# Modulation products on TensorE in pairs of tiles, in the state space stage of a two-layer trunk

## The chip, the cores and the metric

The kernel runs on one core of one Trainium2 chip. The metric is the device time of one execution in microseconds, of which the median over several runs is compared. Engines are called as the profile calls them: PE is TensorE's matmuls and PEld its weight loads, DVE is VectorE, ACT is ScalarE, POOL is GpSimd, and SP is SyncE, whose queue issues most of the DMAs.

## What is computed

Two layers over 256 latent tokens of width 1024, with 256 context tokens that layer 0 reads. All of it is in float32. Layer 0 mixes tokens with a bidirectional state space scan (Mamba-2), layer 1 with a convolution module; each is followed by a gated feed-forward part. Ahead of every part the tokens are normalised and modulated by vectors that come from a condition `c`:

```
def ada_params(sc, w, b):          # sc = silu(c)
    mod = sc @ w + b               # (1, 1024) @ (1024, 6144)
    return [t[:, None, :] for t in jnp.split(mod, 6, axis=-1)]

for i in range(DEPTH):
    sh1, s1, g1, sh2, s2, g2 = ada_params(sc_lat, ada_w[i], ada_b[i])
    xn_lat = modulate(rmsnorm(h_lat, norm_mix_g[i]), sh1, s1)   # h * (1 + scale) + shift
    y_lat = ssd_mixer(...) if i == 0 else conformer_conv_module(...)
    h_lat = h_lat + g1 * y_lat
    h_lat = h_lat + g2 * swiglu(modulate(rmsnorm(h_lat, norm_ffn_g[i]), sh2, s2), ffn_w_in[i], ffn_w_out[i])
```

In the state space mixer `h @ w_in` gives a gate z, the inputs x, B and C of the scan, and its steps dt. x, B and C pass a short convolution and SiLU; then eight groups of four heads each are scanned, and the result goes through the gate, a norm and `w_out`.

The six vectors of a layer have 1024 values each; one vector is the product of silu(c) with a 1024x1024 block of `ada_w`.

## The kernel before, in words

Every large matmul is done in three passes over operands split into a high and a low part (`mm3`, L281 to L283). A weight tile of 128x1024 (or 128x768) comes through `weights` (L266): SP's queue loads it into a raw buffer `wraw`, ACT casts it to the high part `wh` (L273), DVE subtracts to get the low part `wl` (L274), and PE multiplies both. The raw buffers are a ring of four (`wr`, WR = 4), the pairs `wh` and `wl` a ring of four as well. A raw buffer of a weight tile is free when the subtraction is done.

The kernel is a sequence of stages: the modulation of the first norm and the first projections (`ssd_in`, to about 56 us), the state space stage (`ssd`, to about 285 us), the projection through `w_out`, the feed-forward part, the convolution module, and the second feed-forward part.

In the state space stage the eight groups are worked off with one group's projection ahead of the scan of the group before. A group's projection is four weight tiles of `w_xb`; every second group also takes four tiles of `w_z`, every fourth four tiles of `w_c`. A `w_xb` tile feeds 18 matmuls of 128x512, a `w_z` or `w_c` tile 12. The scan of a group loads 1.5 MB of decays (`emat`, L873) and 0.5 MB more (`eo`, L878), works on them on ACT and DVE, and uses products on halves of PE's columns (L951, L959).

The vectors that are needed after this stage are computed inside it, as background work. `self.bg` holds three of them (the mixer's gate, and shift and scale of the feed-forward part; `vector` with `on_pe`). Each call of `weights` adds `self.rate` to a credit, and whenever the credit reaches one, `background` takes one step of the list. A step of `vector` loads one tile of 128x1024 of `ada_w` into a buffer of the same ring `wr` (L344), and multiplies it as it is, in float32, by silu(c) (`ada_mm`, L330): four matmuls, each with 32 columns of stationary values and 256 columns of the tile, at four places beside each other in PE's columns (`tile_position=(0, 32 * j)`). They add up in a bank `pa` over the eight tiles of a vector; then ACT copies the bank out (L316), PE transposes it and DVE adds the bias (L324). The trace has two records for each of these float32 matmuls. A raw buffer of a modulation tile is free when its four matmuls are done. With 0.6 for the rate, the 24 tiles of the three vectors are spread over 40 weight tiles.

In stage 1 the function `quarter` uses the same `ada_mm` (tiles named `araw`) on loads that hold two values of k, with 128 columns for each matmul. Its products for k and k + 1 stand behind each other.

No order is written out by hand for this stage: a scheduler places the instructions of each engine by priority and readiness, with the loads of `ada_w` and of weights raised by 100 (`high_priority(AHEAD)`).

Of the kernel before, what the change touches and what calls it, by code (L numbers as in the profile page):

```python
# [8 lines left out]
F32 = mybir.dt.float32  # L9
# [7 lines left out]
P = 128  # L17
D = 1024
KD = D // P
# [203 lines left out]
class Trunk:  # L223
# [101 lines left out]
                                    in1=bias.rearrange("p (j q) -> p j q", j=4), op=ALU.add)  # L325
        return col

    def ada_mm(self, pa, k, rhs, n):
        for j in range(4):
            self.nc.tensor.matmul(out=pa[32 * j:32 * j + 32, 0:n], lhsT=self.sc[:, k, :], rhs=rhs(j),  # L330
                                  start=k == 0, stop=k == KD - 1, tile_position=(0, 32 * j))

    def vector(self, l, i, on_pe):


        nc, t = self.nc, self.t
        c = PC_AB + l * 48 + i * KD
        bias = self.pc[:, c:c + KD]
        if on_pe:
            pa = self.pa.tile([P, 512], F32, name="pa")  # L340
            for k in range(KD):
                raw = self.wr.tile([P, 1024], F32, name="wraw")
                with self.tc.high_priority(AHEAD):
                    nc.sync.dma_start(out=raw, in_=t["ada_w"][l, k * P:(k + 1) * P, i * D:(i + 1) * D])  # L344
                self.ada_mm(pa, k, lambda j: raw[:, j * 256:j * 256 + 256], 256)
                if k < KD - 1:
                    yield
            col = self.ada_columns(pa, 256, 1, bias)
        else:
            if self.srow is None:  # L350
                self.silu_row()
            col = self.sb.tile([P, KD, 1], F32, name="ada_col", bufs=12)
            for k in range(KD):
                raw = self.ar.tile([P, 1024], F32, name="araw")
                with self.tc.high_priority(AHEAD):
                    nc.sync.dma_start(out=raw, in_=t["ada_wt"][l * 6 + i - 5, k])
                self.flight.append((raw, col, k, (l, i, bias) if k == KD - 1 else None))

                if len(self.flight) >= AR:
                    self.land()  # L360
                yield
            return
        self.done(l, i, col)
        yield
# [456 lines left out]
    def ssd(self, es, xh, xl):  # L821
        nc, t, tc = self.nc, self.t, self.tc
        pd, pa0 = self.ssd_in(xh, xl)
        self.bg = [self.vector(0, i, True) for i in range(2, 5)]
        self.rate = 0.6
        sp_ = es.enter_context(tc.tile_pool(name="ssd", bufs=1))
        sqacc = sp_.tile([P, 2, L], F32, name="sqacc")
        nc.gpsimd.memset(sqacc, 0.0)
# [406 lines left out]
```

## Time and profile before

| what | value |
|---|---|
| median of 3 runs | 884.21 us (881.93 to 885.55) |
| the profiled execution: its own time | 882.65 us |
| its span, first to last instruction | 880.8 us |
| mean granted clock of PE | 0.991 |
| bytes moved | 194.59 MB, 221 GB/s |
| tiles of `ada_w` that come through the ring | 24, 512 KB each, median 4.1 us from issue to landing |

A row of a group of instructions names line, engine, operation and what it writes and reads (out<-in by the program's names, the moving operand first), then how many, and in ns the duration of one. A row of the order of time has start and duration in us and a count of records that were merged. A row of waits says who waited for whom, how long in total, how often, and the longest. SPq is SP's queue of DMA issues. Ends of matmuls are modelled in the trace, so a later start behind a record says more than its end.

### The profile page before, as it was taken

The page shows a single profiled execution, that of the slowest core. Times are in us where ns is not written, and L with a number is a line of the kernel's source. Part 1 is how long each engine was busy: PE and PEld are TensorE (multiplying, and loading weights), DVE is VectorE, ACT ScalarE, POOL GpSimd, SP SyncE. Part 2 cuts the span into 40 slices and gives each one's busy share as a digit, 9 for nine tenths or more (in the row PEclk, how much of TensorE's full clock was granted, in tenths as well). Part 3 has the DMA queues.
Part 4 walks back from the last instruction along what each step waited for, and adds up shares of the span by engine and source line. Part 5 has one row for each costly group of instructions (what it writes and reads, how often), then busy time and mean ns, then how long its engine had stood idle before and what let it go on. Part 6 is the DMA issues. An engine that isn't in the chain of part 4 may idle for free.

```text
span 880.8 us, 12563 instructions
## 1 busy us (share of the span) xinstructions
PE 845.3 (96%) x4555; PEld 645.0 (73%) x4555; DVE 663.6 (75%) x1093; ACT 506.8 (58%) x852; POOL 49.9 (6%) x78
## 2 busy tenths in 40 slices
PE   6999999999999999989999999999989999999996
PEld 3676766767677777767888877877767788888885
DVE  2469588896878989889889888668987896555434
ACT  3376887796767978467244444566354645444421
POOL 1001001101010010120000000010000000000000
PEclk8999999999999999999999999999999999999998
DMA  9747856657563454468899889836655697555521
GB/s 346 312 144 245 288 167 216 239 159 246 157 203 127 161 191 146 160 215 275 288 395 382 333 292 346 286 108 227 169 167 169 220 329 264 182 177 190 191 72 48
DMA packets 55873, 194.59 MB, mean 221 GB/s; under 512 B 6666, under 2 KB 9170, under 8 KB 54787
## 3 DMA queue, kind: packets, MB, share of 16 engines
q1 hardware_dynamic: 54338, 190.00, 62.9%
q0 software_dynamic: 896, 2.28, 0.7%
q10 hardware_dynamic: 576, 1.51, 0.5%
q8 instruction: 36, 0.59, 0.3%
q14 instruction: 27, 0.21, 0.1%
HBM read 191.94 MB, written 1.82 MB: 220 GB/s over the span
## 4 chain that ended last, share of the span: by engine, by line
PE 46%; DVE 4%; DMA 3%; ACT 3%; issue 1%; POOL 0%; SPq 0%; POOLq 0%; ACTq 0%; DVEq 0%
PE acc L283 14%; PE acc L282 14%; PE acc L281 14%; DVE wl L274 2%; PE ps L250 2%; DMA wraw<-in_ffn_out_dram 2%; DMA wraw<-in_w_pw_dram 1%; ACT wh L273 1%; PE ps L1094 1%; ACT modv L147 1%; DMA wraw<-in_ffn_in_dram 1%; ACT nrm L94 0%; DVE araw L370 0%; DVE xml L287 0%; DVE nrm L107 0%
## 5 line engine op out<-in xcount | busy, mean ns | idle before, releaser
L274 DVE TENSOR_TENSOR wl<-wraw,wh 128x1024 fp32r<-128x1024 f32 (+2 forms) x230 | 270.3, 1181 | 99.7 <-ACT wh L273 98.7
L273 ACT CAST wh<-wraw 128x1024 fp32r<-128x1024 f32 (+2 forms) x230 | 232.0, 1017 | 167.5 <-PE acc L283 63.0
L281 PE MATMUL acc<-wh,xmh 128*128 128x512 f32 x544 | 219.2, 403 | 2.4 <-ACT bx L704 1.7
L283 PE MATMUL acc<-wh,xml 128*128 128x512 f32 x544 | 214.9, 395 | 0.4 <-DVE xml L287 0.4
L282 PE MATMUL acc<-wl,xmh 128*128 128x512 f32 x544 | 214.9, 395 | 0.4 <-DVE wl L274 0.4
L281 PEld LDWEIGHTS acc<-wh,xmh 128*128 128x128 f32 x544 | 102.5, 188 | 30.8 <-issue 5.2
L283 PEld LDWEIGHTS acc<-wh,xml 128*128 128x128 f32 x544 | 102.4, 188 | 24.7 <-DVE xml L287 2.0
L282 PEld LDWEIGHTS acc<-wl,xmh 128*128 128x128 f32 x544 | 102.6, 189 | 21.8 <-DVE wl L274 1.0
L281 PE MATMUL acc<-xmh,wh 128*128 128x512 f32 (+1 forms) x200 | 80.7, 403 | 0.0
L282 PE MATMUL acc<-xml,wh 128*128 128x512 f32 (+1 forms) x200 | 79.2, 396 | 0.0
L283 PE MATMUL acc<-xmh,wl 128*128 128x512 f32 (+1 forms) x200 | 78.8, 395 | 0.3 <-DVE wl L274 0.3
L711 DVE SCALAR_TENSOR_TENSOR bx<-bxraw,pc,bx 128x508 f32<-128x508 f32 (+1 forms) x96 | 67.7, 742 | 5.9 <-ACT bx L704 5.7
L282 PE MATMUL acc<-wl,midh 128*128 128x512 f32 x176 | 69.5, 395 | 0.4 <-DVE wl L274 0.3
L283 PE MATMUL acc<-wh,midl 128*128 128x512 f32 x176 | 69.1, 393 | 0.0
L370 DVE SCALAR_TENSOR_TENSOR araw<-araw,srow 128x1024 f32<-128x1024 f32 x56 | 68.1, 1218 | 1.0 <-DMA araw<-in_ada_wt_dram 0.9
L281 PE MATMUL acc<-wh,midh 128*128 128x512 f32 x176 | 66.1, 395 | 0.4 <-ACT wh L273 0.4
L281 PEld LDWEIGHTS acc<-xmh,wh 128*128 128x128 f32 (+1 forms) x200 | 37.2, 186 | 13.6 <-issue 5.1
L283 PEld LDWEIGHTS acc<-xmh,wl 128*128 128x128 f32 (+1 forms) x200 | 37.1, 186 | 9.7 <-issue 1.2
L282 PEld LDWEIGHTS acc<-xml,wh 128*128 128x128 f32 (+1 forms) x200 | 37.2, 186 | 8.7 <-issue 1.9
L282 PEld LDWEIGHTS acc<-wl,midh 128*128 128x128 f32 x176 | 33.0, 188 | 9.5 <-DVE wl L274 2.1
L281 PEld LDWEIGHTS acc<-wh,midh 128*128 128x128 f32 x176 | 32.9, 188 | 8.2 <-ACT wh L273 1.0
L283 PEld LDWEIGHTS acc<-wh,midl 128*128 128x128 f32 x176 | 33.0, 188 | 7.3
(203 smaller groups left out, 1063.0 us busy)
## 6 DMA issues: line engine op xcount, KB each, us to landing
wraw<-in_ffn_in_dram SPq DMA_DIRECT2D x88, 512.0 KB, 5.0
araw<-in_ada_wt_dram SPq DMA_DIRECT2D x56, 512.0 KB, 5.0
wraw<-in_ffn_out_dram SPq DMA_DIRECT2D x44, 512.0 KB, 3.8
wraw<-in_w_xb_dram SPq DMA_DIRECT2D x32, 384.0 KB, 3.9
wraw<-in_ada_w_dram SPq DMA_DIRECT2D x24, 512.0 KB, 4.1
emat<-edram SPq DMA_DIRECT2D x8, 1536.0 KB, 7.8
wraw<-in_w_pw_dram SPq DMA_DIRECT2D x24, 512.0 KB, 4.5
araw<-in_ada_dram SPq DMA_DIRECT2D x16, 512.0 KB, 7.8
```

Of the source, the lines that this page charges most:

```text
L147: j = self.nc.scalar.activation(out=v[:, i], in_=y, func=AF.Identity, scale=g, bias=b)
L250: self.nc.tensor.transpose(out, in_, self.ident[0:n, 0:n])
L273: nc.scalar.copy(out=wh[:r, :n], in_=raw[:r, :n])
L274: nc.vector.tensor_tensor(out=wl[:r, :n], in0=raw[:r, :n], in1=wh[:r, :n].bitcast(F32), op=ALU.subtract)
L281: mm(out=out, lhsT=ah, rhs=bh, start=first, stop=False)
L282: mm(out=out, lhsT=ah, rhs=bl, start=False, stop=False)
L283: mm(out=out, lhsT=al, rhs=bh, start=False, stop=last)
L370: self.nc.vector.scalar_tensor_tensor(out=raw, in0=raw, scalar=1.0, in1=self.srow, op0=ALU.mult, op1=ALU.mult, accum_out=col[:, k])
L711: nc.vector.scalar_tensor_tensor(out=o[:, :, a:b], in0=r[:, :, a + d:b + d], scalar=w(k), in1=o[:, :, a:b], op0=ALU.mult, op1=ALU.add)
L1094: nc.tensor.matmul(out=x[32 * g:32 * g + 32], lhsT=dk[:, blk - 1, g * 8 + i], rhs=rows(u4[:, g])[:, r0:r0 + nr, 4 * i:4 * i + 64], start=i ...
```

## The change

A step of the background work in the state space stage now takes two tiles. Both loads are issued behind each other, and the products of both stand behind each other, those of the later tile first. The first and last product of a sum in PSUM are marked accordingly: tile 1 opens the sum and tile 6 closes it. A vector takes four steps instead of eight, and the rate is 0.3 instead of 0.6, so that the 12 steps are spread over the same 40 weight tiles. The ring keeps its four buffers. Lines behind the change are four higher than before.

```
-    def ada_mm(self, pa, k, rhs, n):
+    def ada_mm(self, pa, k, rhs, n, ends=(0, KD - 1)):
         for j in range(4):
             self.nc.tensor.matmul(out=pa[32 * j:32 * j + 32, 0:n], lhsT=self.sc[:, k, :], rhs=rhs(j),
-                                  start=k == 0, stop=k == KD - 1, tile_position=(0, 32 * j))
+                                  start=k == ends[0], stop=k == ends[1], tile_position=(0, 32 * j))
...
             pa = self.pa.tile([P, 512], F32, name="pa")
-            for k in range(KD):
-                raw = self.wr.tile([P, 1024], F32, name="wraw")
+            for kp in range(KD // 2):
+                raw = [self.wr.tile([P, 1024], F32, name="wraw") for _ in range(2)]
                 with self.tc.high_priority(AHEAD):
-                    nc.sync.dma_start(out=raw, in_=t["ada_w"][l, k * P:(k + 1) * P, i * D:(i + 1) * D])
-                self.ada_mm(pa, k, lambda j: raw[:, j * 256:j * 256 + 256], 256)
-                if k < KD - 1:
+                    for a in range(2):
+                        k = 2 * kp + a
+                        nc.sync.dma_start(out=raw[a], in_=t["ada_w"][l, k * P:(k + 1) * P, i * D:(i + 1) * D])
+
+                for a in (1, 0):
+                    self.ada_mm(pa, 2 * kp + a, lambda j: raw[a][:, j * 256:j * 256 + 256], 256, (1, KD - 2))
+                if kp < KD // 2 - 1:
                     yield
...
         self.bg = [self.vector(0, i, True) for i in range(2, 5)]
-        self.rate = 0.6
+        self.rate = 0.3
```

## The prediction

> **What bounds the kernel now.** I read the busy times of the page first, then the window of the stage that the change touches, then the order of time inside it, and last who waits there.
>
> ```profile
> PE 845.3 (96%) x4555; PEld 645.0 (73%) x4555; DVE 663.6 (75%) x1093; ACT 506.8 (58%) x852; POOL 49.9 (6%) x78
> core 0: us, PE busy (x) PEld busy (x) DVE busy (x) ACT busy (x) POOL busy (x), PEclk, DMA share, GB/s
> 56.00:285.00 229.00, 224.38 (x1266) 161.59 (x1265) 185.94 (x329) 173.92 (x322) 18.09 (x16) 1.00 0.63 204
> ```
>
> TensorE is busy for 96% of the span. From 56 to 285 us, the stretch of the state space stage that holds the products of the change, it is busy 224.38 of 229 us at full clock (PEclk 1.00), so only 4.62 us are idle. VectorE is busy 81% of it, ScalarE 76%, the DMA engines 63%. TensorE is the bound, and what shortens its queue shortens the stage as long as the others keep up. A busy TensorE need not be at its peak, so the next view is its order of time around one run of modulation products; the columns are start, duration, instruction and count.
>
> ```profile
> 59.12 0.39 PE L282 MATMUL acc<-wl,xmh 128*128 128x512 f32 x1
> 59.35 0.40 PE L283 MATMUL acc<-wh,xml 128*128 128x512 f32 x1
> 59.68 0.64 PE L330 MATMUL pa<-wraw,sc 128*32 128x256 f32 x8
> 60.24 0.50 PE L281 MATMUL acc<-wh,xmh 128*128 128x512 f32 x1
> 60.58 0.39 PE L282 MATMUL acc<-wl,xmh 128*128 128x512 f32 x1
> ```
>
> The matmuls of a projection start 0.23 us apart (59.12 to 59.35). One modulation tile, four products in the code and eight records in the trace, each on a quarter of the array's columns, stands between 59.35 and 60.58, which is 1.23 us. Two ordinary steps would be 0.46 us. A run therefore costs 1.23 - 0.46 = 0.77 us.
>
> How much of that is the products themselves?
>
> ```profile
> L330 PE MATMUL pa<-wraw,sc x192: 379/391/403, 59.7 to 257.0; 128*32 128x256 f32 x192
> ```
>
> The first numbers are the shortest, median and longest in ns. Eight records of 0.39 us fit into 0.64 us, so they run side by side; the last starts 0.64 - 0.39 = 0.25 us after the first. They come as two packs of four, one pack each 0.25 us. Two packs are 0.50 us, and 0.77 - 0.50 = 0.27 us is the price of going from the whole array to quarters and back, paid once for each run, whatever its length.
>
> Stage 1 has longer runs, which tell whether the packs keep their pace.
>
> ```profile
> 28.64 0.39 PE L281 MATMUL acc<-xmh,wh 128*128 128x512 f32 x1
> 28.95 0.64 PE L330 MATMUL pa<-araw,sc 128*32 128x128 f32 x16
> 29.53 0.50 PE L282 MATMUL acc<-xml,wh 128*128 128x512 f32 x1
> 29.87 0.40 PE L283 MATMUL acc<-xmh,wl 128*128 128x512 f32 x1
> L330 PE MATMUL pa<-araw,sc x256: 272/273/423, 14.6 to 46.3; 128*32 128x128 f32 x128
> ```
>
> Here two tiles' products (k and k+1 of one load) follow each other: sixteen records, four packs of half the columns. The last pack starts 0.64 - 0.27 = 0.37 us after the first, 0.12 us a pack, which is 0.25 us for 256 columns: the same pace. And the whole run costs 29.87 - 28.64 - 0.46 = 0.77 us, as much as the run above with the same number of columns. Number of instructions and of tiles cost nothing; columns and runs do.
>
> **The change, part by part.** In TensorE's queue, at the first two modulation tiles, there stood in the kernel before (pa is the sum in PSUM, wraw the loaded tile, sc SiLU of the condition):
>
> ```order
> L281 MATMUL acc<-wh,xmh 128x512
> L282 MATMUL acc<-wl,xmh 128x512
> L283 MATMUL acc<-wh,xml 128x512
> L330 MATMUL pa<-wraw,sc 32x256 x4
> L281 MATMUL acc<-wh,xmh 128x512
> ```
>
> and the same again 24 matmuls later. In the changed kernel the first place is closed, and at the second stands:
>
> ```order
> L281 MATMUL acc<-wh,xmh 128x512
> L282 MATMUL acc<-wl,xmh 128x512
> L283 MATMUL acc<-wh,xml 128x512
> L330 MATMUL pa<-wraw,sc 32x256 x8
> L281 MATMUL acc<-wh,xmh 128x512
> ```
>
> Both tiles moved to the place of the later one. Over the stage the before has 26 such runs for its 24 tiles (two tiles are cut in two by other work), the changed kernel 13 for its 12 pairs (one is cut, 5 and 3). No product is added or taken away, and the 16 runs of the scan's own half-array products are as many as before. So TensorE loses 26 - 13 = 13 changes to quarters and back.
>
> Sum on TensorE: 13 x 0.27 = 3.5 us. The price has two ends. Were the packs of the second tile spaced like an ordinary matmul, 0.23 us, a run's own price would be 0.77 - 0.46 = 0.31 us, 4.0 us in all; at a pace of 0.25 us it is the 3.5 us. I take 3.6 us, near the second, since the longer runs in stage 1 show that pace.
>
> Where the saved time goes next is decided by TensorE's waits in this stage.
>
> ```profile
> engine line waited for: us in total, times, longest us
> PE acc L281 <- ACT bx L704: 1.7, 3, 0.9
> PE ps L250 <- DVE steps L653: 1.1, 1, 1.1
> PE ps L921 <- ACT btok L917: 0.8, 1, 0.8
> PE ps L250 <- ACT cconv L704: 0.7, 2, 0.5
> PE acc L283 <- DVE wl L274: 0.3, 1, 0.3
> PE ps L951 <- ACT h L923: 0.2, 1, 0.2
> ```
>
> The wait for the scan's steps (L653, at 72 us) hangs on a chain on VectorE that starts from the products of stage 1, and does not move with the runs; one run fewer stands ahead of it, so 0.27 us come back as a longer wait there. That leaves 3.6 - 0.3 = 3.3 us. The waits for ScalarE, 1.7 + 0.8 + 0.7 + 0.2 = 3.4 us, are for copies of what TensorE itself has made; they move along with it, and I cost them at nothing. But the scheduler has dealt ScalarE's and VectorE's queues anew in this stage, so these waits may go altogether (3.4 us gained) or be doubled (3.4 us lost).
>
> The loads are the other part. A raw tile takes one of the four buffers of the ring through which all weights come, until TensorE has multiplied it. On SP's queue, in the part that loads the first modulation tiles (w_c and w_z are projection weights), before:
>
> ```order
> L266 DMA wraw<-in_w_c_dram 128x1024
> L344 DMA wraw<-in_ada_w_dram 128x1024
> L266 DMA wraw<-in_w_c_dram 128x1024 x2
> L344 DMA wraw<-in_ada_w_dram 128x1024
> L266 DMA wraw<-in_w_c_dram 128x1024
> ```
>
> and now:
>
> ```order
> L266 DMA wraw<-in_w_c_dram 128x1024 x3
> L346 DMA wraw<-in_ada_w_dram 128x1024 x2
> L266 DMA wraw<-in_w_c_dram 128x1024
> L266 DMA wraw<-in_w_z_dram 128x1024 x2
> L346 DMA wraw<-in_ada_w_dram 128x1024 x2
> ```
>
> The first load of a pair has moved back past two weight loads, the second has kept its place; no other queue is passed. Then two buffers of four are held at once, and the loads behind a pair wait for it.
>
> ```profile
> SPq L266 <- DVE wl L274: 78.1, 26, 11.3
> SPq L266 <- PE pa L330: 37.5, 13, 6.2
> SPq L344 <- PE pa L330: 37.4, 10, 6.9
> wraw<-in_w_xb_dram SPq DMA_DIRECT2D x32, 384.0 KB, 3.9
> wraw<-in_w_z_dram SPq DMA_DIRECT2D x16, 512.0 KB, 4.4
> L273 ACT CAST wh<-wraw x47: 814/842/1092, 58.9 to 288.8; 128x768 fp32r<-128x768 f32 x26, 128x1024 fp32r<-128x1024 f32 x21
> L274 DVE TENSOR_TENSOR wl<-wraw,wh x46: 944/960/1226, 55.1 to 279.9; 128x768 fp32r<-128x768 f32 x24, 128x1024 fp32r<-128x1024 f32 x22
> ```
>
> SP waits for this ring already, 23 times for modulation products. A freed buffer gives usable weights after the landing, a cast and a subtraction: for a w_xb tile 3.9 + 0.84 + 0.96 = 5.7 us (the medians of cast and subtraction), for a w_z tile, which is larger, 4.4 + 1.09 + 1.23 = 6.7 us (the longest of each). TensorE reaches the third tile behind a pair after two tiles of 12 or 18 matmuls: 24 x 0.23 = 5.5 us to 36 x 0.23 = 8.3 us, and more where transposes or scan products stand between. With the price of the tightest case (6.7 - 5.5 = 1.2 us) the bound is 1.2 us for each of 12 pairs, the other bound nothing, since two buffers stay free. TensorE waited 0.3 us once for wl in the stage before, with the same ring almost as often held; I take nothing. If that cover goes, the row of wl grows.
>
> Sum: 3.3 us less. The profiled execution took 882.65 us, span 880.8 us, so it would take 879.4 us. The runs of before have their median at 884.21 us, 1.6 us above; on that footing the forecast is 884.21 - 3.3 = 880.9 us. About 0.5%, 4.4 us, is what a measurement of this kernel can tell from no change, so the forecast lies just inside it.
>
> **The rivals.** *More than forecast, below 879.8 us.* The forecast's mechanism, with the run price at its upper end (4.0 us) and ScalarE's waits gone: 4.0 + 3.4 = 7.4 us, 876.8 us. For it speaks that ScalarE's queue in the changed program has two table loads fewer; against it, that ScalarE is not the bound.
>
> *Eaten elsewhere, 884 us.* The runs go, but TensorE waits longer for copies that ScalarE and VectorE deliver at their own pace: 3.4 us back, no change. VectorE's 81% speak for it, TensorE's dense queue against it.
>
> *The ring starves TensorE, slower.* Each of the seven groups in which pairs run has its 1.5 MB load of decays, and a weight tile that has to wait for a pair may land behind it.
>
> ```profile
> emat<-edram SPq DMA_DIRECT2D x8, 1536.0 KB, 7.8
> ```
>
> Such a tile is ready 7.8 + 0.84 + 0.96 = 9.6 us after its buffer came free, 1.3 us late against the 8.3 us above, for w_z 10.1 us against 5.5, 4.6 us late. Taken with one late tile of 1.3 us in each group: 7 x 1.3 = 9.1 us lost, 3.6 saved, 889.7 us. It decides once the distance on TensorE is under 9.6 us. Against it: the same loads stand in the queue now, and cost TensorE 0.3 us.
>
> *The second tile's packs wait for the first's.* All packs use the same rows of the array, and each needs its weights loaded.
>
> ```profile
> L330 PEld LDWEIGHTS pa<-wraw,sc x192: 106/108/109, 59.7 to 256.8; 128*32 128x32 f32 x192
> ```
>
> If these 0.11 us could not run under matmuls in flight, each further pack would cost a whole matmul and a load, 0.39 + 0.11 = 0.50 us, and the second tile of a pair 1.0 us where its own run cost 0.77 us. Then 12 x 0.23 = 2.8 us are lost, 887.0 us. In the trace packs of 0.27 us start 0.12 us apart, so loads do run under matmuls of the same rows. The rule is the Trainium skill's, TensorE: Matmul & The Clock Gate, Part 3: Packing small matmuls — row/col tiling: weight loads overlap with matmuls in flight only when the row group differs. The trace disagrees with that.
>
> That the change does not do what it says is ruled out by the order, but for the one cut pair.
>
> **How the numbers follow.** Forecast 0.42; more than forecast 0.30; eaten elsewhere 0.10; waiting packs 0.04; starved ring 0.14. Faster by over 0.5% is the second case, 0.30; slower by over 0.5% the ring, 0.14; the rest is 0.56. The range goes from the end of the second case, 876.8 us, to 886.2 us, which takes in the forecast with ScalarE's waits doubled (884.3 us) and some of the smaller losses on the ring, 2 us; outside are the waiting packs and most of the ring's case.
>
> **What would show it.** In the profile after: 13 runs of modulation products, whole ones of sixteen records, each costing about 0.77 + 0.50 = 1.27 us from the matmul ahead to the second behind it (by the waiting packs 1.8 us); TensorE's busy time in the stage some 3.5 us less and its idle time still under 5 us; the row of TensorE's wait for wl still below 1 us. I am wrong on price if a pair's run costs 1.5 us or more, wrong on cover if TensorE's idle time in the stage grows by over 2 us, wrong on place if the difference lies behind the stage.

## The result and the profile after

| | before | after |
|---|---|---|
| median of 7 runs each, side by side | 885.55 us (881.93 to 887.08) | 891.76 us (889.46 to 893.17) |
| the profiled execution's span | 880.8 us | 887.7 us |
| mean granted clock in it | 0.991 | 0.985 |

The ratio of the times is 1.0079, with an interval of 95% from 1.0058 to 1.0100. The change made the kernel slower by 6 us, where 3.3 us less were forecast and the range ended at 886.2 us.

The page of the profile after shows TensorE as busy as before in sum, in a longer span:

```profile
PE 845.1 (95%) x4555; PEld 649.7 (73%) x4555; DVE 664.6 (75%) x1093; ACT 503.9 (57%) x850; POOL 48.6 (5%) x78
```

**The saving is there.** The order of time around the first pair (start, duration, instruction, count):

```profile
64.72 0.39 PE L283 MATMUL acc<-wh,xml 128*128 128x512 f32 x1
65.04 1.07 PE L330 MATMUL pa<-wraw,sc 128*32 128x256 f32 x16
66.04 0.50 PE L281 MATMUL acc<-wh,xmh 128*128 128x512 f32 x1
66.38 0.40 PE L282 MATMUL acc<-wl,xmh 128*128 128x512 f32 x1
```

From the last matmul ahead to the second behind are 66.38 - 64.72 = 1.66 us; less two ordinary steps of 0.23 us, a pair costs 1.20 us, where two single tiles cost 1.54 us (twice the 0.77 us of the prediction). Twelve pairs save 12 x 0.34 = 4.1 us.

**More was lost to waits.** Two windows from 56 us to the same piece of work, the first product of w_out, of before and then of after (columns as in the prediction's windows, TensorE alone):

```profile
56.00:320.98 264.98, 258.97 (x1454) 1.00 0.62 201
```

```profile
56.00:325.72 269.72, 256.04 (x1454) 0.99 0.60 198
```

The same 1454 records take 2.93 us less of TensorE's time, and yet they end 4.74 us later: its idle time is 13.68 us in place of 6.01. TensorE's waits in the stage of the changed kernel, from 56 to 295 us (engine, line, waited for; total, times, longest):

```profile
PE ps L925 <- DVE xw L915: 5.8, 2, 3.3
PE acc L281 <- ACT bx L708: 2.5, 2, 2.1
PE ps L925 <- ACT btok L921: 1.8, 2, 1.1
PE ps L250 <- DVE steps L657: 1.4, 1, 1.4
PE acc L281 <- ACT zbuf L871: 0.9, 1, 0.9
```

The first row is new in this stretch (behind it both kernels have one such wait of about 1 us, at 301 and 305 us). L925 is a group's first scan product, and it waits for VectorE's xw. The row of the wait for wl, which the prediction wanted watched, has gone altogether.

**How a late weight tile becomes a wait for xw.** The first of the two waits, in views of both kernels. SP's queue in the changed one, with a count of records merged:

```profile
88.10 0.59 SPq L877 DMA_DIRECT2D emat<-edram  x1
92.39 1.54 SPq L346 DMA_DIRECT2D wraw<-in_ada_w_dram  x2
94.03 7.20 SPq L266 DMA_DIRECT2D wraw<-in_w_xb_dram  x2
```

A load of decays (`emat`, 1.5 MB) is issued at 88.10 and a pair from 92.39, and only then, at 94.03, the second weight tile of a group (the third one, merged into the same row, goes at about 100.9). The pair keeps its two buffers until its products at 107.84. In the kernel before, the same tile goes at 95.58, and the decays behind it:

```profile
95.58 0.37 SPq L266 DMA_DIRECT2D wraw<-in_w_xb_dram  x1
96.00 0.42 SPq L873 DMA_DIRECT2D emat<-edram  x1
```

The times of the two kernels are not aligned: what the tile has to be ahead of, a block of work on VectorE, starts at 102.37 in the changed kernel and at 104.25 in the one before. So the tile is issued 8.3 us ahead of the block now and was issued 8.7 us ahead of it before, hardly a difference. What differs is how long it takes to land behind the decays and the pair. The issue of this one tile, after and then before (the last figure is the time from issue to landing):

```profile
wraw<-in_w_xb_dram SPq DMA_DIRECT2D x1, 384.0 KB, 7.9
```

```profile
wraw<-in_w_xb_dram SPq DMA_DIRECT2D x1, 384.0 KB, 4.5
```

It lands at about 102.0. From 101.07 ACT copies the sums of the group before, and casts the tile only behind these copies:

```profile
101.07 0.59 ACT L707 COPY bxraw<-acc 128x512 f32<-128x512 f32 x1 [1.19 <-PE acc L283]
105.02 0.84 ACT L273 CAST wh<-wraw 128x768 fp32r<-128x768 f32 x1
```

VectorE meanwhile:

```profile
99.91 0.96 DVE L274 TENSOR_TENSOR wl<-wraw,wh 128x768 fp32r<-128x768 f32 x1 [0.37 <-ACT wh L273]
102.37 4.84 DVE L715 SCALAR_TENSOR_TENSOR bx<-bxraw,pc,bx 128x508 f32<-128x508 f32 x7 [1.50 <-ACT bx L708]
112.66 1.28 DVE L915 TENSOR_TENSOR xw<-ps,qc 128x512 f32<-128x512 f32 x2
113.86 1.82 DVE L274 TENSOR_TENSOR wl<-wraw,wh 128x768 fp32r<-128x768 f32 x2
```

From 102.37 it works through the convolution of the group, xf and xw, one block of 11.6 us that ends at 113.94. The group's first weight tile was subtracted ahead of it. The second, whose cast was done at 105.9, in the middle of the block, stands behind it, at 113.86. And TensorE:

```profile
109.65 0.39 PE L282 MATMUL acc<-xml,wh 128*128 128x512 f32 x1
110.33 0.40 PE L282 MATMUL acc<-xml,wh 128*128 128x512 f32 x1
114.00 3.67 PE L925 MATMUL ps<-xw,btok 128*128 128x512 f32 x4 [3.27 <-DVE xw L915]
```

At 109.65 it is already multiplying what needs only the high part of the late tile, and at 110.33 the sixth and last of these has gone. With nothing left it stands 3.27 us before the scan product, until the block on VectorE has come to xw. In the kernel before, VectorE had two tiles ready ahead of the same block:

```profile
98.83 0.96 DVE L274 TENSOR_TENSOR wl<-wraw,wh 128x768 fp32r<-128x768 f32 x1 [1.91 <-ACT wh L273]
101.10 0.96 DVE L274 TENSOR_TENSOR wl<-wraw,wh 128x768 fp32r<-128x768 f32 x1 [1.31 <-ACT wh L273]
104.25 4.83 DVE L711 SCALAR_TENSOR_TENSOR bx<-bxraw,pc,bx 128x508 f32<-128x508 f32 x7 [2.20 <-ACT bx L704]
```

and the 18 matmuls of the second, with six of the next tile's high part, kept TensorE busy until the scan product could go without a wait:

```profile
116.09 0.40 PE L282 MATMUL acc<-xml,wh 128*128 128x512 f32 x1
116.33 1.88 PE L921 MATMUL ps<-xw,btok 128*128 128x512 f32 x4
```

In both kernels xw comes 10.3 us after the block's start. What is missing in the changed one is the work that fills this time. The second wait has the same form, but there the tile is late from its issue on. Two pairs, issued from 148.87 and 161.85, in the end held all four buffers, and no weight tile was loaded between 160.2 and 171.08, when the products of the first pair (at 170.38) had set two buffers free:

```profile
171.08 0.80 SPq L266 DMA_DIRECT2D wraw<-in_w_c_dram  x2
```

In the kernel before, the same tile was issued at 165.58 and subtracted at 171.47, ahead of the block, which began at 174.44. In the changed kernel the block began at 175.77, and the subtraction came behind it, at 187.31. TensorE stood 2.49 us:

```profile
187.45 1.98 PE L925 MATMUL ps<-xw,btok 128*128 128x512 f32 x4 [2.49 <-DVE xw L915]
```

At both places the late tile stands behind a load of decays (88.10 and 166.47) that it stood ahead of in the kernel before (96.00 and 167.81). At the second the held buffers delayed its issue. At the first they hardly did, and the trace shows the queue in its place: decays, a weight tile and the pair stand ahead of it. That these make the landing longer is read from the order of the queue; no run tests it alone.

**The idle time also cost clock.** The changed kernel's windows ahead of, from and behind the 3.27 us (TensorE alone: busy, PEclk, DMA share, GB/s):

```profile
110.00:114.00 4.00, 0.73 (x6) 1.00 0.56 212
114.00:118.00 4.00, 4.00 (x7) 0.57 0.46 134
118.00:122.00 4.00, 4.00 (x22) 1.00 0.69 263
```

At 0.57 the four records of L925 took 3.67 us, where they took 1.88 us in the kernel before: another 1.8 us. So the account to the first product of w_out closes: 7.7 us of idle time and 1.8 us of clock, less the runs, is 4.74 us, which puts the saving on runs at 4.7 us. Of the idle time, counted up to there and less that of before, 5.7 us are waits for xw and 1.8 us waits for ScalarE. The twelve pairs are 4.1 us of it; the tiles that were cut into two runs before lie in the rest.

The remaining 2.1 us of the spans' difference lie far behind the stage. At about 653 us both kernels wait 2.8 us for nrm, and the clock falls behind that in both, further in the changed one. Before, then after:

```profile
650.00:655.00 5.00, 3.11 (x11) 0.84 0.68 224
655.00:660.00 5.00, 4.95 (x21) 0.82 0.48 161
```

```profile
655.90:659.00 3.10, 3.01 (x10) 0.66 0.59 223
659.00:664.00 5.00, 5.00 (x13) 0.50 0.39 139
664.00:669.00 5.00, 5.00 (x22) 0.69 0.46 161
```

The wait is as long in both, so this part is not the pairs' doing in any way that the trace shows.

### The profile page after: what moved, and what is told of

Same layout as the page of the kernel before. It is cut to its first block, busy times and chain, and to the rows that moved or that the text cites. A ratio compares the mean times of both kernels' runs of the same rounds, so it can differ in the third digit from the quotient of the medians.

```text
span 887.7 us, 12549 instructions
## 1 busy us (share of the span) xinstructions
PE 845.1 (95%) x4555; PEld 649.7 (73%) x4555; DVE 664.6 (75%) x1093; ACT 503.9 (57%) x850; POOL 48.6 (5%) x78
## 4 chain that ended last, share of the span: by engine, by line
PE 64%; DVE 15%; ACT 6%; DMA 5%; issue 3%; POOL 1%; POOLq 0%; SPq 0%; DVEq 0%; ACTq 0%
PE acc L283 18%; PE acc L282 18%; PE acc L281 18%; DVE bx L715 4%; DVE wl L274 4%; PE ps L250 3%; ACT wh L273 2%; PE ps L925 2%; DMA wraw<-in_w_xb_dram 2%; DMA wraw<-in_w_z_dram 1%; PE ps L955 1%; DMA wraw<-in_w_pw_dram 1%; POOL yw L969 1%; PE ps L1098 1%; PE ps L963 1%
```

## The experiments

My theory: the two buffers that a pair holds. The rivals: the burst of two loads on SP's queue, the joint products themselves, and the chance of the order that the scheduler makes of it. Code is shown against the changed kernel unless the text says otherwise. Every kernel was compared with the kernel before on its own chip (885.0 us for the first four, 884.2 for the next, 884.1 for the last).

| kernel | median, us | ratio to before (95%) |
|---|---|---|
| loads apart, products together | 892.61 | 1.0070 (1.0046 to 1.0095) |
| loads together, products apart | 896.37 | 1.0112 (1.0085 to 1.0139) |
| changed, five buffers | 885.78 | 1.0016 (0.9999 to 1.0034) |
| before, five buffers | 887.17 | 1.0026 (1.0006 to 1.0045) |
| changed, five buffers, other room | 879.90 | 0.9948 (0.9925 to 0.9970) |
| before, five buffers, other room | 879.09 | 0.9944 (0.9925 to 0.9964) |
| changed, ring of four and one own buffer | 883.46 | 0.9999 (0.9983 to 1.0015) |
| before, three buffers | 911.76 | 1.0317 (1.0283 to 1.0352) |
| changed, five, zeros in the tail | 882.73 | 0.9969 (0.9948 to 0.9990) |
| before, five, zeros in the tail | 883.81 | 0.9995 (0.9977 to 1.0013) |
| changed, pairs shifted | 882.86 | 0.9973 (0.9949 to 0.9996) |
| before, tiles shifted | 884.21 | 1.0011 (0.9996 to 1.0025) |

**Loads apart, products together.**

```
-            for kp in range(KD // 2):
-                raw = [self.wr.tile([P, 1024], F32, name="wraw") for _ in range(2)]
+            for k in range(KD):
+                if k % 2 == 0:
+                    raws = []
+                raw = self.wr.tile([P, 1024], F32, name="wraw")
+                raws.append(raw)
...
+                for a in (1, 0) if k % 2 else ():
+                    self.ada_mm(pa, k - 1 + a, lambda j: raws[a][:, j * 256:j * 256 + 256], 256, (1, KD - 2))
...
-        self.rate = 0.3
+        self.rate = 0.6
```

> Loads one by one, one in each step as in the kernel before (rate 0.6), products of both tiles together at every second step as in the changed kernel: 13 runs. Held buffers (my theory: a pair keeps two of the four raw buffers until its products, the weight tile behind it comes late, VectorE does its convolution batch first and TensorE stands before the scan product): the first tile of a pair is held longer still, so at least as slow as the changed kernel, 890 to 895 us, with waits of the scan product L925 for xw of 2 us and more. Burst (rival: two loads of 512 KB one behind the other on SP's queue delay the weight tile): the burst is gone and the saving of about 4 us on TensorE stays, 881 us. Merged products themselves (rival): as the changed kernel, 891 us, but with no new waits of the scan product.

892.61 us, as slow as the changed kernel, with the same two waits:

```profile
PE ps L925 <- DVE xw L915: 5.5, 2, 3.1
```

So the loss does not need the burst: without it nothing is won. The joint products alone fall as the cause as well, since the waits are those of late weights. Here the second tile of the group is late from its issue on, 102.75, only 3.7 us ahead of the block (106.46), and it too stands behind the decays (98.24). The first tile of a pair is held longer than in the changed kernel, so this does not show that the burst costs nothing there.

**Loads together, products apart.**

```
-                for a in (1, 0):
-                    self.ada_mm(pa, 2 * kp + a, lambda j: raw[a][:, j * 256:j * 256 + 256], 256, (1, KD - 2))
-                if kp < KD // 2 - 1:
-                    yield
+                for a in (0, 1):
+                    self.ada_mm(pa, 2 * kp + a, lambda j: raw[a][:, j * 256:j * 256 + 256], 256)
+                    if a == 0 or kp < KD // 2 - 1:
+                        yield
...
-        self.rate = 0.3
+        self.rate = 0.6
```

> Both loads of a pair together, products of each tile in a step of its own as in the kernel before (rate 0.6): 24 runs or a few more. Held buffers: the second tile keeps its buffer a step longer and no run is saved: 890 to 896 us, TensorE's idle time in the stage near 10 us or more. Burst: the same, 890 to 896 us. Merged products themselves: as the kernel before, 885 us. So this one tells the loading from the multiplying, and the kernel with single loads and joint products tells held buffers from the burst.

896.37 us, just above what held buffers and the burst both allow; with the kernel above, that speaks for the buffers. One wait of L925 for xw stayed, at 189 us. The other is gone, in an order in which that group's xw was ready at 91 us, and a wait for a weight tile stands at 144 us:

```profile
PE ps L925 <- DVE xw L915: 2.5, 1, 2.5
PE acc L281 <- ACT wh L273: 2.1, 1, 2.1
```

**Five buffers, in the changed kernel and in the one before.**

```
-WR, W1, W2 = 4, 4, 4
+WR, W1, W2 = 5, 4, 4
```

The room: `ada_row` and `gate_row` with bufs=1 for 2, `sdt` with 2 for 3, and `ccraw` as a part of `bxraw`'s buffers.

> The changed kernel with five raw buffers for four; the room comes from one buffer less each of ada_row, gate_row and the scan's sdt, and from ccraw sharing bxraw's buffers. Held buffers: the weight tile behind a pair comes a buffer earlier, the long waits of L925 for xw go (both longest under 1 us), and the saving on TensorE shows: 880 to 883 us, at least 3 us under the same kernel before with five buffers. Burst or merged products: a fifth buffer does not change the order on the queue or the products, 889 to 892 us. Should the room taken cost something, it shows in the kernel before with five buffers as well.

> The kernel before with five raw buffers, the room taken from the same places. Held buffers: a single tile leaves three buffers free, and little was lost on the ring before, so 883 to 886 us. By the rivals 885 us too; it is the measure for the changed kernel with five buffers.

The changed kernel gained 6 us on itself, 885.78 us, but it was not 3 us under its partner, only 1.4 us (887.17, itself above the 883 to 886 us expected). Inside the stage it was as expected. Of the waits of L925 for xw 0.2 us are left, and the windows to the first product of w_out (changed, then before, both with five) differ by 3.88 us in favour of the pairs, though five records fewer lie in the shorter one:

```profile
56.00:317.81 261.81, 253.89 (x1450) 1.00 0.61 203
```

```profile
56.00:321.69 265.69, 261.38 (x1455) 0.99 0.61 201
```

Both then lost time at the end of the scan, which runs on beside the products of w_out to some 370 us, where in this order no product of w_out was left to fill the wait for the last group. The changed kernel with five, its order of time and its windows:

```profile
376.84 0.80 PE L281 MATMUL acc<-wh,yh 128*128 128x512 f32 x1 [4.70 <-ACT yh L988]
```

```profile
376.80:381.00 4.20, 4.15 (x12) 0.50 0.00 0
381.00:385.00 4.00, 4.00 (x12) 0.50 0.18 41
```

4.7 us idle, and 8 us at half the clock behind them. The kernel before with five buffers has the same wait of 4.7 us. The next kernels take the room elsewhere; there it is 2.0 us with pairs and 0.2 us without, so it comes with this room and its order, not with five buffers as such.

**Five buffers, other room; and one own buffer for a pair.** `yw` now lies in `h0`'s place, and `ada_row` and `gate_row` again have one buffer each; `sdt`, `ccraw` and `bxraw` are as they were.

```
-            w = pr.tile([P, 2, 256], F32, name="yw")
+            w = pr.tile([P, 2, 256], F32, name="h0")
```

The own buffer, with the same room and a ring of four:

```
-                raw = [self.wr.tile([P, 1024], F32, name="wraw") for _ in range(2)]
+                raw = [self.wr.tile([P, 1024], F32, name="mraw", bufs=1), self.wr.tile([P, 1024], F32, name="wraw")]
```

> The changed kernel with five raw buffers again, but the room from elsewhere: one buffer less each of ada_row and gate_row, and yw in the place of h0; sdt, ccraw and bxraw as they were. The first pair with five buffers lost some 4 us behind the stage, at the end of the scan, where TensorE had no product of w_out left (4.7 us idle at 376 us); in this kernel's order such products are left at that place, as in the kernel before. Held buffers: that wait is gone, no wait of L925 for xw above 1 us in the stage, 880 to 883 us, 3 to 4.4 us under its partner. If pairs cost something that no buffer cures: 885 us or more, level with its partner.

> The kernel before with five raw buffers, the room as in the kernel above (one buffer less each of ada_row and gate_row, yw in the place of h0). Held buffers: single tiles hardly lacked buffers, 884 to 887 us. If a fifth buffer is a gain by itself, 880 to 882 us, and then the changed kernel with five owes nothing to the pairs.

> The changed kernel with a ring of four and one more buffer only for the first tile of each pair, so a pair holds one buffer of the ring, as a single tile does. Held buffers: as with five in the ring, 880 to 883 us, both long waits of L925 for xw gone. Burst: both loads stand behind each other on SP's queue as in the changed kernel, 889 to 892 us. Scheduler's chance in the new order: anything from 881 to 892 us, with other waits.

With other room the changed kernel took 879.90 us and the kernel before 879.09 us: both are faster than the kernel before, by 0.5%, and level with each other. So five buffers with this room are a gain without any pair, which I had written down as a possibility but not expected, and the 3 to 4.4 us under the partner did not come. By what I had written, the changed kernel with five then owes nothing to the pairs. What part of the 0.5% is the ring's and what the room's no run separates. The long waits for xw are gone; one of 1.1 us at 152 us stayed, a little over the 1 us expected. The own buffer gave 883.46 us, just above what was expected and 8 us under the changed kernel, with one wait for xw of 1.6 us left. It does not test the burst, since its two loads are mostly 3 us and more apart (for example at 91.1 and 99.1 us). The first product of w_out came 3.2 us earlier with pairs than without (five buffers, changed and before):

```profile
318.22 0.48 PE L281 MATMUL acc<-wh,yh 128*128 128x512 f32 x1
```

```profile
321.43 0.48 PE L281 MATMUL acc<-wh,yh 128*128 128x512 f32 x1
```

In the changed kernel's profile most of it was given back at the scan's end, with 1.97 us of idle time at 373.56 us and then

```profile
373.50:384.00 10.50, 9.75 (x27) 0.53 0.40 144
```

At the last product of w_out it was 0.6 us ahead (390.62 against 391.20 us). Yet the two profiled executions ended 3.0 us apart in its favour (spans of 878.1 and 881.1 us): the partner's, at 882.85 us, was the slowest of its seven. So these two profiles do not show why the medians are level.

**Three buffers in the kernel before.** `WR = 3`, with no pair anywhere.

> The kernel before, no pairs, with a ring of three: while a modulation tile is held two buffers are left, as behind a pair in the changed kernel, and no run is saved. Held buffers: the loss of the changed kernel without its gain, 6.2 + 4.4 = 10.6 us above before, 892 to 898 us, with waits of L925 for xw of 2 us and more where the changed kernel has them. If pairs cost by their loads or products and not by what they hold: 885 to 888 us.

911.76 us, 28 us above before, above the 892 to 898 us expected and much more than the stage's part. Up to the first product of w_out (332.99 us against 320.98) it was 12.0 us late, near the 10.6 us expected; the rest was lost behind, in stages that have no such modulation tiles. The waits in the stage were for wl and wh themselves, and none for xw, where I had expected waits of 2 us and more:

```profile
PE acc L282 <- DVE wl L274: 5.2, 4, 4.0
PE acc L281 <- ACT wh L273: 4.1, 3, 1.5
```

So one buffer less for the weights costs about what all the pairs cost in the stage, but in another way: here the row of wl, the prediction's alarm, does show it. This kernel tells nothing of the block on VectorE.

**Zeros in the tail.** In both kernels with five buffers and the other room, against the same without zeros:

```
             for p2 in range(2):
                 for tt in range(2):
                     c0 = (g % 2) * 256 + p2 * P
                     self.transpose(pz[:, p2, tt * P:tt * P + P], zs[:, tt, c0:c0 + P])
+            if g == GROUPS - 1:
+                self.warm(8, self.bank())
```

> The changed kernel with five raw buffers and the room from ada_row, gate_row and yw, and eight products of zeros of 128x512 (bf16) on TensorE behind the last group's transposes, ahead of the last products of w_out. Nothing uses them. In the kernel without them TensorE stood 1.97 us at 373.56 us there, the granted clock then was 0.50 for some 8 us, and this gave back what the stage had saved. If the drop is brought on by that idle time: idle there under 0.5 us, clock 1.00 from 373 to 390 us, 3 to 4 us less than without them, 876 to 877 us. If the tail is bound by the last group's chain on ACT and DVE alone: 879 to 880 us, no change.

> The kernel before with five raw buffers, the room from the same places, and the same eight products of zeros. It had only 0.17 us idle at the place, but 0.69 and 0.80 us just behind, and a clock of 0.80 and 0.73 there. The zeros cost at most their 8 x 0.21 = 1.7 us and may save the drop: 878 to 880 us. If pairs save 3.3 us in the stage and the tail no longer takes them back, this kernel is 2.5 to 4 us above the changed one with the zeros; if pairs save nothing, both are level.

In the profile of the changed one the drop is gone:

```profile
374.00:378.00 4.00, 2.69 (x15) 1.00 0.57 152
378.00:382.00 4.00, 4.00 (x19) 1.00 0.69 269
```

and the execution that was profiled took 877.86 us, close to the forecast. But the median of its 12 executions, from 877.33 to 883.78 us, was 882.73 us, and that of the other 883.81 us: no gain, and both above what was expected. In the profile of the other, the slowest of its 12 at 886.30 us, the clock was still 0.50 from 382 to 386 us. Of the executions without a profile only the mean clock is known. Nor does the full clock need the zeros: in the shifted kernel below, which has none, it stayed at 1.00 from 374 to 390 us. Whether the tail is what takes the saving back stays open.

**The pairs shifted.**

```
-        self.rate = 0.3
+        self.rate, self.credit = 0.3, 0.75
```

and in the kernel before 0.6 and 0.75.

> The changed kernel with four buffers, its credit begun at 0.75 in place of 0, so that the first pair comes with the first weight tile of the stage, three earlier, and all others follow at the same distances. As many buffers held for as long, but the pairs meet the groups elsewhere; in this order the projection products ahead of the second scan product are as many as in the kernel before. If a held pair costs only where the late weight tile meets VectorE's convolution batch: the 3.3 us wait near 114 us goes, 884 to 888 us. If every pair starves the ring wherever it falls: 889 to 893 us. If the loss was the scheduler's chance: 881 us or so, all of the saving.

> The kernel before with its credit begun at 0.75: the first modulation tile comes one weight tile earlier, the rest as far apart as ever. It shows how much the time moves by such a shift alone: 883 to 888 us if single tiles are insensitive to where they fall; 889 us or more, with a wait of L921 for xw, if the order alone can cost as much as the pairs did.

With four buffers, as many pairs and no room taken, the changed kernel took 882.86 us, 0.27% under before (0.04 to 0.51%) and 9 us under itself. Of the waits for xw this was left:

```profile
PE ps L925 <- DVE xw L915: 0.4, 1, 0.4
```

The kernel before moved by nothing that can be measured, 884.21 us. So that every pair starves the ring is wrong, and so is that a burst costs by itself: the pairs' loads stand behind each other here too (81.4 and 82.2, 94.0 and 94.4 us). A pair costs where the weight tile behind it comes too late for VectorE's block, and in the changed kernel two pairs fell so. In the shifted kernel, and in the changed ones with five buffers in the ring, the tiles in question stand ahead of the decays again. That the held buffers put them behind, and not the scheduler's choice alone, is shown for the second wait and argued for the first; the two theories are not told apart further. 882.86 us lies between what I had written for the one and the other.

**What the pairs are worth where the ring isn't starved** can be read from four couples that differ by the pairs alone: -1.4, +0.8, -1.1 and -1.4 us in their medians, on average -0.8 us. The 95% intervals of the two kernels of each couple overlap or touch, so none shows a gain for certain. In the stage the saving shows in the profiles (3.9, 3.2 and 2.7 us earlier at the first product of w_out in the three couples with five buffers, 0.4 us in the shifted one, which waits 2 us more than its partner before that). The profiled executions with pairs end 2.2 to 8.4 us earlier; the medians show less of it. What takes the rest back, and in which executions, isn't shown.

## Why the prediction was wrong

*The price of a run* was right: 1.20 us for a pair against 1.27 forecast, 4.1 us saved for 3.6, just over the upper bound of 4.0. *The second pack's weight loads* do run under matmuls: the four packs of a pair, 0.39 us each, start within 1.07 - 0.39 = 0.68 us, and a pair at 1.20 us is far from the 1.8 us of that rival. The rule of the Trainium skill that stood beside it (TensorE: Matmul & The Clock Gate, Part 3) does not hold for these products. *The steps' wait* grew from 1.1 to 1.4 us, by the 0.3 us written down.

*ScalarE's waits* did not simply move along. Those for bx and btok went from 2.5 to 4.3 us, 0.9 us for zbuf came, and 0.9 us for cconv and h went: 1.8 us more, inside the bounds of 3.4 us either way, on the wrong side of the value taken.

*The ring* is the step that failed: "I take nothing". In the profile it cost 5.8 us of waits for xw and 1.8 us of clock behind them, more than the runs saved. Two mistakes are in it. The first is in the path from a freed buffer to usable weights. I added landing, cast and subtraction, 5.7 to 6.7 us, as if the DMA queue, ACT and VectorE were there at once. At the first wait 19.8 us passed from the tile's issue to the start of its subtraction (94.03 to 113.86); in the kernel before it was 5.5 us (95.58 to 101.10). The landing took 7.9 us in place of 4.5, the cast came 3 us later, behind ACT's copies, and the subtraction stood behind the block of 11.6 us from the convolution to xw that VectorE works through for a group. A tile that misses its place ahead of the block by a little is late by nearly the whole block. The distance on TensorE, 5.5 to 8.3 us, does not cover 11.6 us.

The second mistake is the row that I named as the alarm. I expected a starved ring to show as TensorE's wait for wl. It showed as a wait for xw, since TensorE's order already puts the scan product ahead of the products that need the late wl; the row for wl even fell to nothing.

The rival "the ring starves TensorE" thus had the right resource, and its link, a weight tile behind the decays' load, is there at both waits. But it left out ACT's copies and VectorE's block, and took 1.3 us in each of seven groups where two groups waited 3.3 and 2.5 us. That its 889.7 us lies near the 891.76 us measured is in part luck. Its 0.14 was too little. A ring for which SP's queue waited 23 times for modulation products, on a VectorE that is 81% busy, was a poor ground for a price of nothing.

*The clock* was in no term. I priced an idle microsecond as one; behind 3.27 us of idle time came 1.8 us more.

The check "wrong on cover if TensorE's idle time in the stage grows by over 2 us" was the right one to write down. It grew by 8.1 us (4.62 in 229 us before, 12.72 in 234 us after):

```profile
56.00:290.00 234.00, 221.28 (x1264) 163.91 (x1263) 188.35 (x330) 171.61 (x321) 16.32 (x16) 0.99 0.62 201
```

## What to carry to other kernels

Work that is bunched to save a switch holds its buffers longer: price that in buffers of the ring and not only in time on the engine that is saved. For a tile that comes later, look at what stands on each engine of its path just then; where an engine works through a long block, as VectorE did for 11.6 us here, a delay of a microsecond can become one of nearly the whole block, and the wait shows up at another instruction. Look at what stands ahead of the tile in the DMA queue, too. Where a shift by a few steps moves the time by more than the change itself (9 us here against 4), try the change at several shifts before judging it.

## What was not expected of the hardware

TensorE's clock fell behind idle times that I had taken for harmless, and not behind all of them. In these traces 3.27 us were followed by a clock of 0.57 over 4 us and 4.70 us by 0.50 for 8 us, but behind 2.49 us (at 187.45 us) the clock stayed at 1.00, while it fell to 0.53 over 10.5 us behind 1.97 and 0.69 us with two matmuls between them. The Trainium skill, TensorE: Matmul & The Clock Gate, Part 1, says that the array falls to half its clock after an idle window of some 3.4 us that runs freely, so that the place in the window matters. The 4.70 us and the half clock agree with that; the drop behind 1.97 and 0.69 us, in which TensorE was not idle for a whole window, is more than this says.

One kernel's executions differ by more than the change is worth, and in part the clock goes with it: the seven of the changed kernel with five buffers and other room run from 876.05 us at a mean clock of 0.991 to 882.08 us at 0.983, though another of them took 879.90 us at 0.983. A saving of 3 us is smaller than this spread.
